# A branch projection of a macaron block as seven block products, with its weight sums made in DRAM

## The chip, the cores and the metric

One core of a Trainium2 chip runs the whole block in one launch. The metric is the device time in microseconds, as the median of several executions. The engines are named as the profile names them: PE multiplies matrices, ACT and DVE work on tiles in SBUF and PSUM, POOL here mostly clears tiles and issues a few transfers, SP issues nearly all transfers. Each engine, and each queue of transfers, takes its instructions in the order of the program.

## The reference

A layer on 256 tokens of width 1024: a gated feed-forward part, a mixer, a cross attention to 256 memory tokens, and a second feed-forward part, all in float32. The change touches the end of the mixer:

```python
o_a = rmsnorm(o_a.astype(x.dtype), hg_norm_g[l]) * jax.nn.silu(g_a)
y_a = o_a @ w_branch_a[l]
...
y_b = o_b.astype(x.dtype) @ w_branch_b[l]

gate = jax.nn.sigmoid((gates + b_gate[l]).astype(jnp.float32)).reshape(B, S, N_BRANCH, D)
y = (gate[:, :, 0] * y_a.astype(jnp.float32) + gate[:, :, 1] * y_b.astype(jnp.float32)).astype(x.dtype)
x = x + rmsnorm(y @ w_out[l], mix_post_g[l])
```

`o_a` and `o_b` are 256 x 1024, both branch matrices 1024 x 1024.

## The kernel before

**Weights.** Every matrix is cut into units of 128 x 1024 numbers (512 KB), two blocks of 128 x 512 each; a matrix of 1024 x 1024 has eight. `load_split` (L138) takes one unit through three steps: SP loads it into one of four `raw` tiles, ACT rounds it to `hi` (L147, the line of the cast), DVE takes `lo = raw - hi` (L149). There are eight `hi` and eight `lo` tiles. A product of float32 accuracy is made of three matmuls per block: hi times hi, hi times lo, lo times hi (`proj_tok`, L223). A weight tile comes free when PE has used it last, a `raw` tile when DVE has taken its `lo`.

**Order.** The kernel is written as one long sequence, but a list scheduler decides the order on each engine: by when operands are expected, by the number of buffers, and by marks in the code (`issue_after`, and `after(i)`, which ties work to the i-th matmul in a log). Once built, the order is fixed: an instruction that waits holds up all behind it on its engine.

**PSUM** has four `acc` banks, two `mm` banks and two `tr` banks of 128 x 512.

**The stages around the change, in PE's order.**

- `f_a`, `q_a` and so on (L844 on): the columns of the input projection. Before them `row_of` (L351) sends a column of norm factors through DRAM as a row and back to all partitions: two transfers on POOL (L356, L358); the row is first used on DVE at L861.
- `gates(c)` for c = 0 to 3 (L1252): the two branches' gates. Each chunk c has four units and, for the two halves h of the tokens, 24 matmuls into an `mm` bank, which DVE evicts into `zg` with a scale and the bias row `brow` (L1261). In the gaps of chunks 0 and 1 PE transposes the first branch's tokens into `OA` and makes the attention output `OB` (`fox_out`, L1222; its last split is the mark `OB`).
- `memT`, the memory tokens transposed, is scaled and split by eight ACT and eight DVE instructions (L366, L367).
- The sigmoid of the four gates (L1294), after the mark `OB`, in place; then `table`, which loads the ACT functions of the later stages.
- The branch loop (L1308): for c = 0, 1 (half of the output's columns) the first branch (`br_a` with `OA`), then the second (`br_b` with `OB`), each for both halves h: four units, twice 24 matmuls, 192 in all. DVE multiplies each `mm` bank by its gate (L1320) and adds the second branch to the first (L1323). `y_T` transposes the sum on PE and splits it, 16 matmuls (`L_Y`) into a later product.
- `rows_proj` (L1325) for `w_out`.

Other parts of the kernel (the feed-forward parts) already compute with seven block products.

Of the kernel before, what the change touches and what calls it, by code (L numbers as in the profile page):

```python
# [59 lines left out]
HX = T + 2 * KB  # L60

WARM = 8

X_AT = 12

# [17 lines left out]
def block_kernel(ctx: ExitStack, tc: tile.TileContext, wts, head_in, gf_in, x_in, mem_in, memT_in, cols, rows, fbias, masks, out):  # L83
# [12 lines left out]
    def MM(*args, **kw):  # L96
        log.append(PE.matmul(*args, **kw).ins)  # L97
# [9 lines left out]
    def nm(s):  # L107
        count[0] += 1
        return f"{s}_{count[0]}"

    def m4(shape, dt=F32, n="m"):
        return mp.tile(shape, dt, tag="m4", name=nm(n))
# [19 lines left out]

    place = {}

    def parts_of():
        return [wp.tile([P, D], F32R, tag=t, name=nm(t), bufs=8) for t in ("hi", "lo")]

    def load_split(src, n=512, behind=None, parts=None):  # L138

        raw = wp.tile([P, D], F32, tag="raw", name=nm("raw"), bufs=4)  # L140
        hi, lo = parts or parts_of()
        r, h, l = raw, hi, lo
        if n < 512:
            r, h, l = (p.rearrange("p (k n) -> p k n", k=2)[:, :, :n] for p in (raw, hi, lo))
        loads.append(nc.sync.dma_start(r, src).ins)
        with tc.issue_after(behind[0]) if behind else nullcontext():
            S.copy(h, r)  # L147
        with tc.issue_after(behind[1]) if behind else nullcontext():
            V.tensor_tensor(out=l, in0=r, in1=h.bitcast(F32), op=ALU.subtract)  # L149
        return hi, lo  # L150

    def unit(name, i):
        u = _AT[name] + i
        if u not in cache:
            cache[u] = load_split(wts[u - 4], behind=hold.get(u), parts=place.get(u))
        return cache[u]

    def chunk(name, c):
        return [unit(name, 4 * c + i) for i in range(4)]

    def blk(units, kb, n=512):
        hi, lo = units[kb // 2]
        o = (kb % 2) * 512
        return hi[:, o : o + n], lo[:, o : o + n]
# [124 lines left out]
    def table(ins):  # L289

        with tc.issue_after(ins):
            S.activation(warm, ones[:, 0:1], AF.Abs_reciprocal_sqrt)
# [461 lines left out]

    X1 = Joined()
    heads, raw1 = [], []
    for kb in range(KB):
# [492 lines left out]
    def gates(c):  # L1252
        u = chunk("gates", c)
        z = m4([P, 2, 512], n="zg")
        brow = wp.tile([P, D], F32, tag="extra", name=nm("brow"), bufs=4)[:, :512]
        with tc.issue_after(loads[-1]):
            nc.sync.dma_start(brow, rows[4 + c // 2, c % 2 * 512 : c % 2 * 512 + 512].partition_broadcast(P))
        for h in range(2):
            ps = mm()
            proj_tok(ps, X2, u, h)  # L1260
            V.scalar_tensor_tensor(out=z[:, h], in0=ps, scalar=r2[h], in1=brow, op0=ALU.mult, op1=ALU.add)  # L1261
        zs.append(z)
# [11 lines left out]
            fox_out(g)  # L1274


    memT_s = [m4([P, 4, T], n="memT") for _ in range(2)]
    for j in range(2):
        nc.sync.dma_start(memT_s[j], memT_in[:, 4 * j : 4 * j + 4, :])
# [9 lines left out]
    rowm = row_of(fac[1])  # L1289
    for c in range(2, 4):  # L1290
        gates(c)
    for c in (0, 2, 1, 3):
        with tc.issue_after(marks["OB"][0]):
            z_last = S.activation(zs[c], zs[c], AF.Sigmoid)  # L1294
    table(z_last.ins)
    g2 = load_row(1)
    Y = Pair()

    def y_T(c, h, m):

        tr = trp()
        with after(m):
            for i in range(4):
                PE.transpose(tr[:, i * P : (i + 1) * P], zs[c][:, h, i * P : (i + 1) * P], ident)
            hs = slice(h * P, (h + 1) * P)
            split(Y.h[c][:, :, hs], Y.l[c][:, :, hs], tr.rearrange("p (i t) -> p i t", i=4))

    for c in range(2):  # L1308
        for name, X, zc in (("br_a", OA, c), ("br_b", OB, 2 + c)):
            u = chunk(name, c)  # L1310
            for h in range(2):
                z = zs[zc][:, h]
                m = len(log)
                ps = mm()
                proj_tok(ps, X, u, h)
                if zc != c and h == 1:
                    y_T(c, 0, m + L_Y)
                if zc == c and h == 0 and c:
                    y_T(c - 1, 1, m + L_Y)
                V.tensor_tensor(out=z, in0=ps, in1=z, op=ALU.mult)  # L1320
                if zc != c:
                    za = zs[c][:, h]
                    V.tensor_tensor(out=za, in0=za, in1=z, op=ALU.add)  # L1323

    def rows_proj(ps, X, name, h, kbs, cols=(0, 1)):  # L1325
        a, b = h * P, h * P + P
# [246 lines left out]
```

## Time and profile before

| | us |
|---|---|
| median of three executions | 774.62 |
| lowest, highest | 774.27, 776.5 |
| the profiled execution | 776.3 |
| its span, first to last instruction | 774.0 |
| PE busy in the span | 764.9 |
| DVE busy | 647.6 |
| ACT busy | 493.2 |

The granted TensorE clock of the profiled execution was 0.998 of full speed. A share of busy time is an average over all stages; what a stage is bound by is read from that stage's window, and from what its engines waited for. In rows of groups the columns are busy time, mean ns of one, and idle time of the engine just before such instructions, with what ended most of it; in the timeline they are start, duration, instruction, and in brackets the idle time before it.

### The profile page before, as it was taken

To read this page: it belongs to the slowest core of one execution; us is meant where nothing else is said; L and a number is where in the kernel's file an instruction comes from. 1 tells how busy PE (TensorE), PEld (TensorE's weight loads), DVE (VectorE), ACT (ScalarE), POOL (GpSimd) and SP (SyncE) were. 2 spreads that over 40 slices of the span, in tenths; PEclk is the share of its full clock that TensorE was granted. 3 is DMA by queue.
4 is the path that set the end of the run, shared out by engine and by line. 5 is a ranking of instruction groups with operands and counts; after the bars stand their busy time and mean duration, and the time that the engine had idled before them with its cause. 6 is when DMAs were issued, how large, how long until landed. Compare 5 with 4: busy or idle time off the path is not lost.

```text
span 774.0 us, 11823 instructions
## 1 busy us (share of the span) xinstructions
PE 764.9 (99%) x4394; PEld 650.7 (84%) x4394; DVE 647.6 (84%) x992; ACT 493.2 (64%) x803; POOL 17.3 (2%) x39
## 2 busy tenths in 40 slices
PE   9999999999999999999999999999999999999996
PEld 8888888888888998898888888889888888888885
DVE  7798999997778898988776665886578999999993
ACT  7656564768775678557676444862668557665762
POOL 0000000000000101200000000000000000000000
PEclk9999999999999999999999999999999999999999
DMA  9748377255654545834667655456075736467241
GB/s 344 264 165 284 151 261 272 88 188 206 220 177 147 166 155 155 308 111 160 221 245 246 203 173 174 164 173 233 9 248 183 271 113 202 182 213 303 76 142 55
DMA packets 44505, 148.06 MB, mean 191 GB/s; under 512 B 5144, under 2 KB 8864, under 8 KB 44448
## 3 DMA queue, kind: packets, MB, share of 16 engines
q1 hardware_dynamic: 43168, 144.83, 54.0%
q0 software_dynamic: 848, 2.12, 1.1%
q8 instruction: 34, 0.56, 0.3%
q10 hardware_dynamic: 432, 0.37, 0.2%
q14 instruction: 23, 0.19, 0.1%
HBM read 146.24 MB, written 1.06 MB: 190 GB/s over the span
## 4 chain that ended last, share of the span: by engine, by line
PE 83%; DVE 9%; ACT 3%; DMA 2%; issue 1%; DVEq 0%; ACTq 0%; SPq 0%
PE mm L97 37%; PE acc L97 34%; PE tr L97 10%; DVE lo L149 3%; DMA raw<-in_wts_dram 2%; DVE lo L168 1%; ACT hi L147 1%; PE tr L379 1%; PE tr L438 1%; DVE k L986 1%; DVE qf L986 1%; ACT hi L167 1%; DVE xs L415 0%; ACT f L1024 0%; PE tr L1210 0%
## 5 line engine op out<-in xcount | busy, mean ns | idle before, releaser
L149 DVE TENSOR_TENSOR lo<-raw,hi 128x1024 fp32r<-128x1024 f32 (+1 forms) x212 | 251.5, 1202 | 36.9 <-ACT hi L147 31.7
L147 ACT CAST hi<-raw 128x1024 fp32r<-128x1024 f32 (+1 forms) x212 | 215.5, 1035 | 76.8 <-PE mm L97 38.0
L97 PE MATMUL mm<-hi,hlT 128*128 128x512 f32 (+1 forms) x624 | 190.5, 382 | 0.0
L97 PEld LDWEIGHTS mm<-hi,hlT 128*128 128x128 f32 x624 | 115.3, 188 | 19.8
L97 PE MATMUL mm<-lo,hlT 128*128 128x512 f32 (+1 forms) x312 | 117.5, 381 | 0.1
L97 PE MATMUL acc<-hi,act 128*128 128x512 f32 x352 | 113.3, 390 | 0.0
L97 PEld LDWEIGHTS acc<-hi,act 128*128 128x128 f32 x352 | 66.1, 188 | 13.6 <-ACT act L167 0.2
L97 PE MATMUL acc<-lo,act 128*128 128x512 f32 x176 | 69.3, 394 | 0.0
L167 ACT CAST hi<-sraw 128x1024 fp32r<-128x1024 f32 x50 | 52.0, 1055 | 27.0 <-DVE sraw L578 21.3
L97 PEld LDWEIGHTS mm<-lo,hlT 128*128 128x128 f32 x312 | 58.5, 188 | 10.0 <-DVE lo L149 0.5
L97 PE MATMUL acc<-hlT,hi 128*128 128x512 f32 x256 | 64.4, 393 | 0.0
L168 DVE TENSOR_TENSOR lo<-sraw,hi 128x1024 fp32r<-128x1024 f32 x50 | 60.3, 1219 | 0.5 <-ACT hi L167 0.4
L97 PEld LDWEIGHTS acc<-hlT,hi 128*128 128x128 f32 x256 | 46.1, 189 | 8.3
L97 PE MATMUL mm<-hlT,hi 128*128 128x512 f32 (+1 forms) x192 | 43.9, 357 | 0.0
L97 PE MATMUL tr<-hi,sx 128*128 128x512 f32 x120 | 39.3, 391 | 0.0
L97 PEld LDWEIGHTS acc<-lo,act 128*128 128x128 f32 x176 | 33.1, 188 | 7.2 <-DVE lo L149 0.7
L97 PEld LDWEIGHTS acc<-hlT,lo 128*128 128x128 f32 x256 | 35.0, 190 | 2.5
L97 PEld LDWEIGHTS mm<-hlT,hi 128*128 128x128 f32 x192 | 33.2, 189 | 4.3
L97 PE MATMUL acc<-hlT,lo 128*128 128x256 f32 x256 | 36.2, 283 | 0.0
L578 DVE TENSOR_TENSOR sraw<-sraw,raw 128x1024 f32<-128x1024 f32 x30 | 35.9, 1219 | 0.1
L97 PE MATMUL tr<-hlT,hi 128*128 128x512 f32 x128 | 32.6, 394 | 0.5 <-DVE act L168 0.5
L97 PE MATMUL mm<-hlT,lo 128*128 128x256 f32 x160 | 28.0, 285 | 1.1 <-DVE lo L149 1.1
(293 smaller groups left out, 1279.0 us busy)
## 6 DMA issues: line engine op xcount, KB each, us to landing
raw<-in_wts_dram SPq DMA_DIRECT2D x227, 512.0 KB, 4.3
sraw<-in_wts_dram SPq DMA_DIRECT2D x20, 512.0 KB, 5.5
raw<-in_gf_dram SPq DMA_DIRECT2D x12, 344.0 KB, 3.8
head<-in_head_dram SPq DMA_DIRECT2D x7, 392.0 KB, 6.6
grow<-in_rows_dram SPq DMA_DIRECT2D x4, 512.0 KB, 5.2
xs<-in_x_dram SPq DMA_DIRECT2D x2, 512.0 KB, 7.8
cbm<-cd POOLq DMA_DIRECT2D x2, 512.0 KB, 6.9
brow<-in_rows_dram SPq DMA_DIRECT2D x4, 256.0 KB, 3.7
```

The costliest lines, as they stand in the source:

```text
L97: log.append(PE.matmul(*args, **kw).ins)
L147: S.copy(h, r)
L149: V.tensor_tensor(out=l, in0=r, in1=h.bitcast(F32), op=ALU.subtract)
L167: a = S.copy(hi, src)
L168: b = V.tensor_tensor(out=lo, in0=src, in1=hi.bitcast(F32), op=ALU.subtract)
L379: PE.transpose(blocks[-1][1], src(kb), ident)
L438: PE.transpose(trv[:, j, h * P : (h + 1) * P], ats[c, h][:, j * P : (j + 1) * P], ident)
L578: V.tensor_tensor(out=x, in0=x, in1=y, op=ALU.add)
L986: V.tensor_tensor(out=tv, in0=tv, in1=other, op=ALU.mult)
```

## The change

The first branch's product, 256 x 1024 by 1024 x 1024, is taken as 2 x 2 blocks: tokens in halves (h), the contraction in halves (k), output columns in halves (c). Write x(h,k) for the four blocks of `o_a` and b(k,c) for those of the matrix. Instead of eight block products of 12 matmuls (two contracted blocks of 128 for each of the unit's two, three matmuls each) there are seven:

- p1 = x00 b00, copied to SBUF by ACT; the same bank then takes x01 b10 on top and is y00.
- p3 = (x01 - x00 + x10 - x11) b11
- q5 = (x10 - x11) s0, with s0 = b00 + b01
- q6 = (x00 - x10 + x11) s4, with s4 = s0 + b11
- p7 = (x00 - x10) s2, with s2 = b01 + b11; the same bank later takes x11 s6 on top, with s6 = s4 + b10
- v = p1 - q6 and w = q5 - v; then y11 = w - p7 (before x11 s6 is added), y01 = w + p3, y10 = v + p7, where y(h,c) has the rows h and columns c of the output.

**Sums of weights.** `plan` makes eight DRAM tiles (two units for each of s0, s2, s4, s6). `background` is called at every weight load; when the number of loads is one of 74, 78, ... 102, SP issues a copy from DRAM to DRAM of the one summand, and POOL a transfer that adds the other to it there, after the copy. s4 copies a finished s0, s6 a finished s4. In the program's order these fall into the stages from the first `f_a` weights to those of the `q_a` and `gf` stages, and `row_of`'s two transfers on POOL stand behind the third of the eight additions, the clearing of `aux` (L908) behind the eighth.

**Combinations of tokens.** After `fox_out`, on DVE: two additions of 128 x 1024 that join hi and lo of `OA`, four subtractions of 128 x 512; then two casts of 128 x 1024 on ACT and two subtractions on DVE for their hi and lo. They lie in two `raw` tiles and four `extra` tiles; `brow` of the gates 2 and 3 moves from `extra` to the pool `z2`.

**The branch loop.** Steps of `branch_pair`, a generator, alternate with the second branch's four products (c, h). The sigmoid of the fourth gate and the `table` load move out of the sigmoid loop, behind the second branch's second product in the text. Units loaded for the first branch go from 8 to 14: b00, b10, b11, s0, s4, s2, s6 with two units each.

```diff
+SUMS_AT = (*range(74, 103, 4),)
...
+    sums, jobs = [], []
+
+    def plan(name):
+        t = dp.tile([8, P, D + 16], F32, name=nm("sums"))
+        sums.extend(t[i, :, :D] for i in range(8))
+
+        def b(k, n, j):
+            return wts[_AT[name] + 4 * n + 2 * k + j - 4]
+
+        for j in range(2):
+            jobs.append((sums[j], b(0, 0, j), b(0, 1, j)))
+            jobs.append((sums[2 + j], b(1, 1, j), b(0, 1, j)))
+        for j in range(2):
+            jobs.append((sums[4 + j], sums[j], b(1, 1, j)))
+        for j in range(2):
+            jobs.append((sums[6 + j], sums[4 + j], b(1, 0, j)))
+
+    def background():
+        if jobs and len(loads) in SUMS_AT:
+            to, x, y = jobs.pop(0)
+            with tc.issue_after(loads[-1]):
+                nc.sync.dma_start(to, x)
+            G.dma_start(to, y, accum_op=ALU.add)
...
         loads.append(nc.sync.dma_start(r, src).ins)
+        background()
...
+    plan("br_a")
     X1 = Joined()
...
-        brow = wp.tile([P, D], F32, tag="extra", name=nm("brow"), bufs=4)[:, :512]
+        if c < 2:
+            brow = wp.tile([P, D], F32, tag="extra", name=nm("brow"), bufs=4)[:, :512]
+        else:
+            brow = sp.tile([P, 512], F32, tag="z2", name=nm("brow"), bufs=3)
...
+    fx, fh, fl = (
+        [wp.tile([P, D], dt, tag=tag, name=nm("fx"), bufs=4).rearrange("p (k t) -> p k t", k=4) for _ in range(2)]
+        for tag, dt in (("raw", F32), ("extra", F32R), ("extra", F32R))
+    )
+    for k in range(2):
+        V.tensor_tensor(out=fx[k], in0=OA.h[k].bitcast(F32), in1=OA.l[k].bitcast(F32), op=ALU.add)
+    fa_, fb_, fd_, fe_ = (fx[k][:, :, h * P : h * P + P] for h in range(2) for k in range(2))
+    V.tensor_tensor(out=fe_, in0=fd_, in1=fe_, op=ALU.subtract)
+    V.tensor_tensor(out=fd_, in0=fa_, in1=fd_, op=ALU.subtract)
+    V.tensor_tensor(out=fa_, in0=fa_, in1=fe_, op=ALU.subtract)
+    V.tensor_tensor(out=fb_, in0=fb_, in1=fa_, op=ALU.subtract)
+    for k in range(2):
+        S.copy(fh[k], fx[k])
+        V.tensor_tensor(out=fl[k], in0=fx[k], in1=fh[k].bitcast(F32), op=ALU.subtract)
+
+    def gated(c, h, x):
+        z = zs[c][:, h]
+        V.tensor_tensor(out=z, in0=x, in1=z, op=ALU.mult)
+
+    def plus(c, h):
+        V.tensor_tensor(out=zs[c][:, h], in0=zs[c][:, h], in1=zs[2 + c][:, h], op=ALU.add)
+
+    def branch_pair():
...
+        p1 = acc()
+        product(p1, of_x(0, 0), plain(0, 0), True)
+        p1s = half_tile("p1")
+        S.copy(p1s, p1)
+        product(p1, of_x(1, 0), plain(1, 0), False)
+        gated(0, 0, p1)
+        yield
+        p3 = acc()
+        product(p3, of(1, 0), plain(1, 1), True)
+        q5 = acc()
+        product(q5, of(1, 1), summed(0), True)
+        yield
+        q6 = acc()
+        product(q6, of(0, 0), summed(4), True)
+        with tc.high_priority():
+            v = less(p1s, q6)
+            w = less(q5, v)
+        p7 = mm()
+        product(p7, of(0, 1), summed(2), True)
+        with tc.high_priority():
+            gated(1, 1, less(w, p7))
+            gated(1, 0, less(w, p3, ALU.add))
+        yield
+        product(p7, of_x(1, 1), summed(6), False)
+        with tc.high_priority():
+            gated(0, 1, less(v, p7, ALU.add))
+            plus(0, 1)
+        yield
...
-    for c in (0, 2, 1, 3):
+    for c in (0, 2, 1):
         with tc.issue_after(marks["OB"][0]):
-            z_last = S.activation(zs[c], zs[c], AF.Sigmoid)
-    table(z_last.ins)
+            S.activation(zs[c], zs[c], AF.Sigmoid)
...
+    pair = branch_pair()
     for c in range(2):
-        for name, X, zc in (("br_a", OA, c), ("br_b", OB, 2 + c)):
...
+        u = chunk("br_b", c)
+        for h in range(2):
+            next(pair)
+            m = len(log)
+            ps = mm()
+            proj_tok(ps, OB, u, h)
+            if h == 1:
+                y_T(c, 0, m + L_Y)
+                if c == 0:
+                    with tc.issue_after(log[-1]):
+                        z_last = S.activation(zs[3], zs[3], AF.Sigmoid)
+                    table(z_last.ins)
+                else:
+                    y_T(0, 1, m + L_Y + 4)
+            gated(2 + c, h, ps)
+            if (c, h) != (0, 1):
+                plus(c, h)
```

`product` takes the three matmuls of each of its four blocks; `of` and `of_x` pick the block of the combined tokens or of `OA`; `summed` loads two units of a sum from DRAM with `load_split`, `plain` two units of the matrix; `less` subtracts (or adds) into a tile of 128 x 512.

More of the change, by code (lines that the diff above doesn't have):

```diff
@@ new lines, in branch_pair, with of, of_x, plain @@
+    def branch_pair():
+        assert not jobs
+        def of(k, h):
+            return lambda kk: (fh[k][:, kk, h * P : h * P + P], fl[k][:, kk, h * P : h * P + P])
+        def of_x(k, h):
+            return lambda kk: (OA.hi(4 * k + kk, h * P, h * P + P), OA.lo(4 * k + kk, h * P, h * P + P))
+        def plain(k, n):
+            return [unit("br_a", 4 * n + 2 * k + j) for j in range(2)]
+        def summed(i):
+            return [load_split(sums[i + j]) for j in range(2)]
+        def product(ps, stat, u, start):
+            for kk in range(4):
+                ah, al = stat(kk)
+                wh, wl = blk(u, kk)
+                for i, (x, y) in enumerate(((ah, wh), (ah, wl), (al, wh))):
+                    MM(ps, x, y, start=start and kk == 0 and i == 0, stop=kk == 3 and i == 2, skip_group_check=not start)
+        def half_tile(n):
+            return sp.tile([P, 512], F32, tag="z2", name=nm(n), bufs=3)
+        def less(x, y, op=ALU.subtract):
+            t = half_tile("br")
+            V.tensor_tensor(out=t, in0=x, in1=y, op=op)
+            return t
+        p1 = acc()
[26 more added lines that the diff above has]
+        yield
@@ L1306, in y_T @@
             split(Y.h[c][:, :, hs], Y.l[c][:, :, hs], tr.rearrange("p (i t) -> p i t", i=4))
+    pair = branch_pair()
     for c in range(2):
-        for name, X, zc in (("br_a", OA, c), ("br_b", OB, 2 + c)):
[L1310 to L1323, printed above, removed]
+        u = chunk("br_b", c)
[15 more added lines that the diff above has]
+                plus(c, h)
     def rows_proj(ps, X, name, h, kbs, cols=(0, 1)):
```

## The prediction

> **What bounds the kernel now.** I read the page's busy times and chain first, then what PE waited for, then the branch stage by windows.
>
> ```profile
> span 774.0 us, 11823 instructions
> PE 764.9 (99%) x4394; PEld 650.7 (84%) x4394; DVE 647.6 (84%) x992; ACT 493.2 (64%) x803; POOL 17.3 (2%) x39
> PE 83%; DVE 9%; ACT 3%; DMA 2%; issue 1%; DVEq 0%; ACTq 0%; SPq 0%
> ...
> engine line waited for: us in total, times, longest us
> PE mm L97 <- DVE lo L149: 1.1, 1, 1.1
> PE tr L97 <- PEq L1562: 0.8, 1, 0.8
> PE tr L97 <- DVE act L168: 0.5, 1, 0.5
> ```
>
> PE is busy for 764.9 of 774.0 us and its listed waits add up to 2.4 us. So the time is the number of matmuls times their pace, as long as nothing else falls behind; and a change can gain little except by dropping matmuls. The stage in question, from the first branch matmul to the first of w_out:
>
> ```profile
> core 0: us, PE busy (x) PEld busy (x) DVE busy (x) ACT busy (x) POOL busy (x), PEclk, DMA share, GB/s
> 170.00:250.00 80.00, 79.94 (x411) 67.73 (x410) 62.55 (x109) 55.05 (x100) 1.73 (x4) 1.00 0.59 194
> 360.00:400.00 40.00, 40.00 (x207) 33.72 (x206) 30.08 (x43) 27.58 (x49) 0.00 (x0) 1.00 0.66 229
> 417.60:461.10 43.50, 43.50 (x199) 35.97 (x198) 26.90 (x29) 19.45 (x20) 0.00 (x0) 1.00 0.58 195
> ...
> 10 pieces in order of time: start us, us, what
> 444.34 16.34 PE mm L97 x72
> ```
>
> From 417.6 to 461.1 PE is full at granted clock 1.00, DVE is busy for 26.9 of 43.5 us. One matmul takes 16.34/72 = 0.227 us, and the two branches' 192 take 43.6, the whole window. The window 360 to 400 is where the operands of the new products are made, 170 to 250 where the sums are made in DRAM.
>
> **What is removed.** Seven products of 12 matmuls replace eight for the first branch: 84 for 96, so 12 x 0.227 = 2.72 us less. PE is full here, so all of it counts: -2.72 us, 0.35 % of the time. That is the whole possible gain.
>
> **What is added: operands.** The new fx work is two additions and two subtractions for the lo part of 128x1024, four subtractions of half that size on DVE, and two casts on ACT. Nearest rows:
>
> ```profile
> L147 ACT CAST hi<-raw 128x1024 fp32r<-128x1024 f32 (+1 forms) x212 | 215.5, 1035 | 76.8 <-PE mm L97 38.0
> L578 DVE TENSOR_TENSOR sraw<-sraw,raw 128x1024 f32<-128x1024 f32 x30 | 35.9, 1219 | 0.1
> ...
> L149 DVE TENSOR_TENSOR lo<-raw,hi 128x1024 fp32r<-128x1024 f32 x33 | 40.1, 1221 | 10.0 <-ACT hi L147 8.8
> L1320 DVE TENSOR_TENSOR zg<-mm,zg 128x512 f32<-128x512 f32 x8 | 5.5, 688 | 8.5 <-PE mm L97 8.5
> L1323 DVE TENSOR_TENSOR zg<-zg,zg 128x512 f32<-128x512 f32 x4 | 2.8, 688 | 0.1
> ```
>
> DVE: 4 x 1.22 + 4 x 0.69 = 7.6 us; ACT: 2 x 1.04 = 2.1. In 360 to 400 DVE has 30.1 of 40 us, so 37.7 with it: it still fits behind PE as a sum, but everything behind it on DVE comes later, and the fx tiles hold two of the four raw buffers meanwhile, so weight loads start later too.
>
> The first thing late is an eviction. In the changed order on ACT and DVE the first half of the third gates chunk is evicted behind two casts, the sigmoid's table, one sigmoid, eight memT activations, a further cast and its subtraction; two mm banks exist, and the fourth chunk's first half needs that bank.
>
> ```profile
> 395.76 0.48 PE L97 MATMUL mm<-hi,hlT 128*128 128x512 f32 x1
> ...
> 396.04 0.59 ACT L167 CAST hT<-acc 128x512 fp32r<-128x512 f32 x1 [0.68 <-PE acc L97]
> 396.65 1.28 ACT L1294 ACT_TABLE_LOAD   x1
> 397.94 2.01 ACT L1294 ACTIVATE zg<-zg 128x1024 f32<-128x1024 f32 x2
> ...
> 399.86 1.69 ACT L366 ACTIVATE hlT<-memT,cols_s 128x256 fp32r<-128x256 f32 x4
> 401.77 1.71 ACT L366 ACTIVATE hlT<-memT,cols_s 128x256 fp32r<-128x256 f32 x4 [0.22 <-DMA memT<-in_memT_dram]
> ...
> 404.09 0.75 DVE L1261 SCALAR_TENSOR_TENSOR zg<-mm,facs,brow 128x512 f32<-128x512 f32 x1
> 404.76 3.49 DVE L149 TENSOR_TENSOR lo<-raw,hi 128x1024 fp32r<-128x1024 f32 x3
> ```
>
> The third chunk starts on PE at 395.76, so the fourth needs its bank 48 matmuls later, at 406.65; before, the eviction ended at 404.84, 1.8 us ahead. In the changed order the last hT cast ends at 396.63, then 2 x 1.04, 1.28, 1.06, 1.69 + 1.71, 1.04, a subtraction of 1.16 (3.49/3) and the eviction of 0.75: 407.4. That is 0.8 us late if the second of the two raw tiles is there; it waits for a raw buffer that fx or the previous chunk's last subtraction gives back at about 394 and lands 4.3 us later, at 398.3, its cast ending at 399.3 for 398.7: 0.6 more. Bounds 0 and 2.1 (memT landing later as well), taken 1.4: +1.4 us.
>
> **What is moved: the last sigmoid.** The sigmoid of the fourth gate chunk and the table load after it now stand on ACT between the casts of the first product's weights, with T the end of the gates on PE (417.6 before).
>
> ```profile
> 413.00 0.75 DVE L1261 SCALAR_TENSOR_TENSOR zg<-mm,facs,brow 128x512 f32<-128x512 f32 x1
> ...
> 418.69 0.75 DVE L1261 SCALAR_TENSOR_TENSOR zg<-mm,facs,brow 128x512 f32<-128x512 f32 x1
> ...
> 413.74 1.05 ACT L147 CAST hi<-raw 128x1024 fp32r<-128x1024 f32 x1 [2.37 <-PE mm L97]
> ...
> 419.47 1.06 ACT L1294 ACTIVATE zg<-zg 128x1024 f32<-128x1024 f32 x1 [0.59 <-DVE zg L1261]
> 420.54 1.28 ACT L292 ACT_TABLE_LOAD   x1
> ```
>
> DVE is through the fourth chunk's first eviction at 413.75, T-3.9. Then it has the other branch's three subtractions (3.5), four short steps of the norm (about 0.7) and the subtraction for the first product's first unit (1.2): done at T+1.5. PE wants it as its third matmul, at T+0.45: about 1.1 late. Behind it come the chunk's last eviction (T+2.3), the sigmoid (T+3.3) and the second unit's cast (T+4.4), wanted as the 15th matmul at T+3.2+1.1: 0.1 late, since PE now mixes the two branches' matmuls. The next unit's cast, the table, another cast and the copy of the first product (0.59) end at T+8.4; PE wants to go on in that bank at the 32nd matmul, T+7.0+1.2: 0.2. Together 1.4; before, the same sigmoid held up nothing, since the first branch's subtractions ran from 404.76 on. Bounds 0 (DVE reaches these subtractions early) and 2.0; taken 1.4.
>
> **The branch stage** has 22 subtractions and about 17 additions, products and splits: 22 x 1.22 + 17 x 0.69 = 38.6 us on DVE for 180 matmuls, 40.8 us; before it was 26.9 for 43.5. ACT's casts go from 16 to 22, 23 of 40.8 us: no bound. PE's weights thus arrive with little in hand, where the other branch's chunk keeps four of the eight hi/lo pairs. Each subtraction queued behind a sum that waits for a product's end can cost up to 1.2; I take 0.3 in all, bounds 0 and 3. The bias rows of the later gates from another pool and the moved transposes of y cost nothing: their number is the same, and the rows land like weights, in some 4 us, with a chunk (10.9 us of PE) in hand; without that cover, a late row would hold the same eviction as above.
>
> **Sums in DRAM.** Eight copies on SP and eight accumulating transfers on POOL, 512 KB each. No row shows either kind. Nearest rows:
>
> ```profile
> q1 hardware_dynamic: 43168, 144.83, 54.0%
> raw<-in_wts_dram SPq DMA_DIRECT2D x227, 512.0 KB, 4.3
> cbm<-cd POOLq DMA_DIRECT2D x2, 512.0 KB, 6.9
> ...
> 166.49 45.80 SPq L145 DMA_DIRECT2D raw<-in_wts_dram  x20
> ...
> 200.24 0.60 POOL L356 DMA_DIRECT2D rd<-runs  x1 [173.40 <-DVE runs L354]
> 204.29 0.56 POOL L358 DMA_DIRECT2D row<-rd  x1 [3.45 <-PE mm L97]
> ...
> 204.84 0.58 POOL L908 MEMSET aux<- 128x256 f32 x2
> ...
> 216.04 0.69 DVE L861 TENSOR_TENSOR f<-f,row 128x512 f32<-128x512 f32 x1
> ...
> L1010 DVE COPY_PREDICATED aux<-masks_s,acc x2: 442/445/448, 262.5 to 262.8; 128x256 f32<-128x256 int32 x2
> ```
>
> A load of 512 KB takes 0.54 x 774 x 0.524/144.83 = 1.5 us of all sixteen engines, so the sixteen transfers take 24 us, and 36 if reading both operands costs half as much again: 0.30 to 0.45 of the 80 us from 170 to 250, where the share is 0.59. Sum 0.89 to 1.04: full at worst, some 3 us of weights later. Half of the idle time ahead of all casts ends with PE (38.0 of 76.8 us on the page), so loads are there ahead of room for them, and I take 0, bounds 0 and 3. Two queues can stick. SP's fifth copy, about 40 us after the first, waits for the first accumulation: issued some 7 us after its copy (6.9 above, the slowest 512 KB row there), it has over 25 us in hand. On POOL the broadcast of the norm's row stands behind the third accumulation, which waits for a copy issued near 195, so it starts near 202 instead of 200.24; DVE needs the row at 216.04, and it landed about 4 us after 204.29: 8 us in hand for 2 lost. The clearing of aux, at 204.84 before, moves behind the last accumulation, near 252, and is wanted at 262.5.
>
> The page "DMA: Bandwidth & Descriptors" of the Trainium skill, section "Issuing engines are not separate DMA queues", says that transfers of any issuing engine run on the same sixteen engines and interleave, which speaks against calling POOL's transfers free; its section on the anatomy of one DMA would put one of 512 KB at 2.0 us + bytes/436e3 = 3.2 us, an estimate, and the sum would be the same.
>
> **Sum:** -2.72 + 1.4 + 1.4 + 0.3 = +0.4 us on the profiled execution's 776.3: 776.7. That execution lies 1.7 above the median 774.62, so on the median's footing 775.0. About 0.3 % (2.3 us) is what a measurement here can tell from no change.
>
> **Rivals.**
> 1. All of it hidden: DVE, with 10 us idle in 360 to 400, takes evictions in time and ACT's casts come early. For it: before, no wait in these stages. Against: 1.8 us in hand at the bank, of which the queue eats more. 774.62 - 2.7 = 771.9. Chance 0.22.
> 2. Slower, DVE becomes the bound of the branch stage: 38.6 of 40.8 us leaves 2.2 for its waits, and it had 8.5 us of them on PE alone in the old order (L1320 above). From 2.2 us of waits on it costs one for one; with half to all of 8.5, 2 to 6 us beside the likeliest case's sum: 777 to 781. Against: waits before came because it had nothing else to do. Chance 0.22.
> 3. Slower, the accumulations: where one takes over about 25 us, SP stops at the fifth copy with loads behind it; where the third is issued 8 us late, DVE stops at the row. Each us beyond that costs one; 3 to 10 give 778 to 785. Against: no 512 KB row is over 7 us. Chance 0.11.
> 4. That the change does not do what it says, with as many matmuls as before, 774.6: excluded, twelve are gone from PE's order.
>
> The page "SBUF — State Buffer" of the Trainium skill, section "Who interferes with whom", lets DVE block GpSimd's writing of transfer descriptors while it runs in its two-port modes; that would make rival 3's accumulations late, and no run here shows it.
>
> **Numbers.** The likeliest case has 0.45, 773.3 to 777. Below 772.3 (faster) lie rival 1 and a little of the likeliest: 0.24; above 776.9 rivals 2 and 3 and a little: 0.35; the rest, 0.41, is the same. The range 771.6 to 779.8 leaves out most of rival 3 and the ends of 1 and 2.
>
> **What would show it.** Branch matmuls over 40.8 us with PE full would bear out the gain. A PE wait on DVE's third-chunk eviction just before the fourth chunk, near 1.4 us, and one of about 1 us on the first product's lo, show the two stalls; if PE has no waits there and the time falls by 2.7, rival 1 is right. DVE busy for over 95 % of the branch stage with several PE waits on lo is rival 2; waits near 170 to 250, rival 3. A fall above 3 us, or a stall elsewhere, would make the working wrong.

## The result, and the profile after

The changed kernel takes 780.36 us in the median (775.13 to 786.21, 13 runs) against 775.5 for the kernel before in runs beside it (774.27 to 777.6, 13 runs): a ratio of 1.0054, 95 % interval 1.0037 to 1.0071. That is slower by about 0.5 %, or 4 us, though twelve matmuls are gone. The times also lie further apart than before, 11 us against 3: the seven executions at a mean granted clock of 0.998 or 0.999 took 775.1 to 780.4 us, the six at 0.993 to 0.996 took 781.0 to 786.2. The profiled execution took 782.04 us, 5.7 more than the profiled one before.

The page of the kernel after, rows as shown of before; in the rows of transfers the last number is us from issue to landing:

```profile
span 780.2 us, 11871 instructions
...
PE 766.4 (98%) x4382; PEld 649.5 (83%) x4382; DVE 663.0 (85%) x1011; ACT 500.8 (64%) x812; POOL 23.7 (3%) x47
...
PE 72%; DVE 11%; DMA 8%; ACT 4%; issue 4%; DVEq 0%; ACTq 0%; SPq 0%
...
L176 ACT CAST hi<-raw 128x1024 fp32r<-128x1024 f32 (+1 forms) x218 | 221.7, 1035 | 80.3 <-DMA raw<-in_wts_dram 46.0
...
raw<-in_wts_dram SPq DMA_DIRECT2D x225, 512.0 KB, 4.4
...
raw<-in_gf_dram SPq DMA_DIRECT2D x12, 344.0 KB, 6.3
sums<-in_wts_dram POOLq DMA_DIRECT2D x8, 512.0 KB, 8.0
...
sums<-in_wts_dram SPq DMA_DIRECT2D x4, 512.0 KB, 8.7
```

Three things are to be seen. PE runs 4382 matmuls instead of 4394 and is yet busy for 1.5 us more: some of them ran at a lower clock. In the chain that ended last, DMA has 8 % where it had 2 %. And the idle time of ACT ahead of the casts, before ended half by PE (38.0 of 76.8 us), now ends with a load in 46.0 of 80.3 us: loads are what comes last.

What PE waited for in the kernel after (us in total, times, longest us):

```profile
PE mm L99 <- ACT hlT L395: 1.3, 1, 1.3
PE acc L99 <- DVE lo L178: 1.2, 2, 0.8
PE mm L99 <- DVE lo L178: 1.0, 2, 0.5
PE tr L99 <- PEq L1680: 0.8, 1, 0.8
PE acc L99 <- DVE q L911: 0.7, 1, 0.7
PE mm L99 <- DVE hlT L396: 0.7, 1, 0.7
PE acc L99 <- DVE qf L1003: 0.5, 1, 0.5
PE mm L99 <- DVE zg L1294: 0.4, 1, 0.4
```

The waits on `hlT`, `q` and `qf` stand in stages whose computation the change does not touch. Comparing the times at which the same matmul starts in the two traces gives, stage by stage, what was lost (us, after less before): to the mixer's start (186) -0.7; to `f_a`'s start (209) +3.7; `f_a` to `gf` 0; the first `gf` stretch (254 to 264) +1.7; to the gates -0.6; gates 0 and +0.6; the branch stage 45.55 for 44.95, +0.6; from w_out to the end +0.8. So 5.4 of the 6.2 us by which the span grew are lost where the sums are made, over 150 us ahead of the branch stage.

Windows of the kernel after on the two lossy stages and the branch stage, then of the kernel before on the first two (columns as in the prediction's windows):

```profile
190.00:212.00 22.00, 20.07 (x85) 15.91 (x84) 14.16 (x26) 14.08 (x26) 2.01 (x3) 0.92 0.78 219
254.00:268.00 14.00, 12.78 (x258) 11.95 (x258) 12.42 (x21) 7.43 (x13) 2.25 (x7) 1.00 0.75 222
422.40:468.00 45.60, 43.87 (x194) 34.48 (x193) 37.40 (x42) 28.77 (x31) 0.81 (x2) 1.00 0.80 276
```

```profile
190.00:212.00 22.00, 21.94 (x104) 17.92 (x103) 17.17 (x29) 17.14 (x33) 1.73 (x4) 1.00 0.69 220
254.00:268.00 14.00, 14.00 (x271) 13.74 (x270) 13.47 (x22) 8.09 (x15) 2.66 (x12) 1.00 0.49 157
```

PE was full in both stretches before. Now it idles 1.93 us in the first and 1.22 in the second, and in the first its mean granted clock is 0.92.

**The first loss, step by step.** The timeline of ACT in the kernel after (start, duration, what, in brackets the idle time before it and what ended it):

```profile
194.17 0.19 ACT L316 ACTIVATION_READ_ACCUMULATOR junk<-xs 128x1 f32 x1
197.13 1.04 ACT L176 CAST hi<-raw 128x1024 fp32r<-128x1024 f32 x1 [2.76 <-DMA raw<-in_wts_dram]
198.08 0.29 ACT L339 ACTIVATE y<-ss,v 128x1 f32<-128x1 f32 x1
198.28 0.28 ACT L340 ACTIVATE v<-ss,v 128x1 f32<-128x1 f32 x1
198.46 0.60 ACT L395 ACTIVATE hlT<-tr,cols_s 128x128 fp32r<-128x128 f32 x2
```

And of PE:

```profile
197.21 0.39 PE L99 MATMUL mm<-hi,hlT 128*128 128x512 f32 x1
198.86 0.74 PE L99 MATMUL mm<-w,hlT 128*128 128x512 f32 x2 [1.26 <-ACT hlT L395]
200.26 4.04 PE L99 MATMUL mm<-w,hlT 128*128 128x512 f32 x10 [0.66 <-DVE hlT L396]
```

The cast at 197.13 is that of `f_a`'s second unit. Its load was issued at 189.86 and landed at 197.1, 7.2 us later where a load takes 4.3 before. PE wants this unit only at 212.9, so the load has over 14 us in hand. But the cast stands in ACT's fixed order ahead of the activations that make `hlT` of the second half of the tokens, and PE wants those at 197.6. ACT waits 2.76 us for data that nobody wants yet, and PE stands still behind it. After that the clock falls, in narrow windows of the kernel after:

```profile
196.00:200.00 4.00, 2.33 (x9) 1.25 (x8) 1.41 (x3) 1.94 (x5) 0.00 (x0) 1.00 0.99 381
200.00:204.00 4.00, 3.74 (x10) 3.01 (x11) 2.75 (x11) 2.45 (x7) 1.42 (x2) 0.62 1.01 302
204.00:206.00 2.00, 2.00 (x9) 1.62 (x9) 0.00 (x0) 0.18 (x1) 0.00 (x0) 0.90 0.78 141
```

The lost clock costs 4 x 0.38 + 2 x 0.10 = 1.7 us; with 1.93 idle that is 3.6 of the stage's 3.7.

**The second loss** has the same form. ACT, then PE, of the kernel after:

```profile
259.00 0.77 ACT L176 CAST hi<-raw 128x688 fp32r<-128x688 f32 x1 [1.31 <-DMA raw<-in_gf_dram]
259.68 0.36 ACT L248 COPY plo<-acc 128x256 f32<-128x256 f32 x1
261.92 0.63 ACT L910 ACTIVATE q<-z 128x512 f32<-128x512 f32 x1 [1.88 <-DVE z L909]
```

```profile
263.33 0.46 PE L99 MATMUL acc<-q,k 128*32 128x32 f32 x32 [0.72 <-DVE q L911]
...
264.59 0.46 PE L99 MATMUL acc<-qf,early 128*32 128x32 f32 x32 [0.49 <-DVE qf L1003]
```

A cast of a `gf` unit waits 1.31 us for its load. Behind it stand the copy `plo`, then over DVE `z`, then the sigmoid `q`, which PE wants. PE waits 0.72 and 0.49 us.

### The profile page after: what moved, and what is told of

Read it like the earlier page. It is cut to its first block, busy times and chain, and to the rows that moved or that the text cites. A ratio compares the mean times of both kernels' runs of the same rounds, so it can differ in the third digit from the quotient of the medians.

```text
span 780.2 us, 11871 instructions
## 1 busy us (share of the span) xinstructions
PE 766.4 (98%) x4382; PEld 649.5 (83%) x4382; DVE 663.0 (85%) x1011; ACT 500.8 (64%) x812; POOL 23.7 (3%) x47
## 4 chain that ended last, share of the span: by engine, by line
PE 72%; DVE 11%; DMA 8%; ACT 4%; issue 4%; DVEq 0%; ACTq 0%; SPq 0%
PE acc L99 30%; PE mm L99 30%; PE tr L99 10%; DMA raw<-in_wts_dram 4%; DVE lo L178 4%; DMA raw<-in_gf_dram 2%; DVE lo L197 2%; ACT hi L176 2%; DMA raw<-sums 1%; PE tr L467 1%; PE tr L408 1%; DVE qf L1016 1%; DVE k L1016 1%; ACT hlT L395 1%; ACT f L1054 0%
## 5 line engine op out<-in xcount | busy, mean ns | idle before, releaser
L178 DVE TENSOR_TENSOR lo<-raw,hi 128x1024 fp32r<-128x1024 f32 (+1 forms) x218 | 258.6, 1201 | 38.0 <-ACT hi L176 34.4
L176 ACT CAST hi<-raw 128x1024 fp32r<-128x1024 f32 (+1 forms) x218 | 221.7, 1035 | 80.3 <-DMA raw<-in_wts_dram 46.0
```

## The experiments

The twelve runs asked three things: what the transfers cost alone and through what (E2, E3, E5, E6, E11), what the branch stage costs without them (E1, E4, E7, E9, E10), and whether the parts add up (E0, E8). Ratios are to the kernel before in runs beside it, with 95 % intervals; stage figures are differences to the kernel before, from one profile each.

**E0, the same kernel again.**

> The changed kernel once more, for its spread. Both theories: about 780 us, ratio 1.004 to 1.007. Transfers theory (the sums' transfers make weight loads late between 186 and 270 us): the profile again shows PE idle for 1 to 3 us between 190 and 210, and again a granted clock under 1.00 right behind it; how much varies from run to run, and with it the time. Branch theory (operand work and the branch stage cost it): PE's loss between 190 and 210 is a chance of one run and is gone here, with the time still near 780.

1.0081 [1.006, 1.0102], 781.98 us. The profiled execution took 786.25 us, the most of its six, and lost at the same two places: +4.3 at `f_a` and +4.5 in `gf`. There the cast waits 2.82 us for its load instead of 1.31, and now the clock falls behind it as well; windows of E0:

```profile
262.00:266.00 4.00, 1.77 (x102) 1.44 (x100) 2.77 (x5) 1.97 (x4) 1.13 (x3) 1.00 0.98 204
266.00:270.00 4.00, 3.29 (x102) 3.10 (x103) 3.96 (x7) 1.41 (x3) 0.00 (x0) 0.57 0.72 207
```

So the loss differs between these two executions with how late the loads land, and a late load that leaves PE idle long enough also costs a stretch at half clock.

**E1, the branch as changed, without the sums in DRAM.** The second, fourth, sixth and seventh products read plain units of the matrix.

```diff
-    plan("br_a")
...
         def summed(i):
-            return [load_split(sums[i + j]) for j in range(2)]
+            w = {0: 0, 4: 2, 2: 4, 6: 6}[i] + _AT["br_a"] - 4
+            return [load_split(wts[w + j]) for j in range(2)]
```

> The changed kernel without its sixteen background transfers; the products that need sums load plain units of the same matrix instead, so the output is not the reference's, and the branch stage has the same loads and matmuls. Transfers theory: 774.5 to 776.5 us, ratio 0.999 to 1.001, with PE full and clock 1.00 between 180 and 270. Branch theory: 779 to 781, unchanged.

1.0012 [1.0, 1.0023]. PE is full from 190 to 212 and both lossy stages are gone (-0.4 and 0). The branch stage takes 45.43 us against 44.95. So without one background transfer the twelve matmuls' 2.72 us still do not appear.

**E2, the kernel before with the sixteen transfers, which nobody reads.** `plan` and `background` are added to the kernel before, and nothing else.

```diff
+SUMS_AT = (*range(74, 103, 4),)
...
         loads.append(nc.sync.dma_start(r, src).ins)
+        background()
...
+    plan("br_a")
     X1 = Joined()
```

> The kernel before with only the sixteen background transfers added, at the same loads; nobody reads the sums. Transfers theory: 779 to 782 us, ratio 1.005 to 1.008, with PE idle between 190 and 210. Branch theory: 775 to 776, ratio 1.000.

1.0038 [1.0023, 1.0053], some 3 us, a little less than the transfers theory gave. The transfers alone cost that, and with E1 it adds up: 0.38 + 0.12 = 0.50 % against 0.54 (0.81 in E0). The profile puts 1.6 of its 2.6 us in the `f_a` stage again. Accumulations took 6.8 us there in the median, copies of a matrix unit 5.4 and copies of a sum 6.6.

**E3, the same transfers at other places,** two groups: under the first feed-forward part, and under the attention and the gates.

```diff
-SUMS_AT = (*range(74, 103, 4),)
+SUMS_AT = (58, 59, 64, 65, 131, 132, 138, 140)
```

> The changed kernel with the sums' transfers at other loads: the first four at loads 58, 59, 64 and 65 (about 115 to 150 us), the others at 131, 132, 138 and 140 (about 337 to 385 us), stretches with DMA shares of 0.2 to 0.5. Transfers theory: 774 to 777 us, ratio 0.998 to 1.002, PE full between 190 and 270. Branch theory: 779 to 781.

1.0064 [1.0046, 1.0083]: no better. `f_a` (-0.4) and `gf` (0) lose nothing, but 1.7 us are lost ahead of 186, 1.7 in the gates, and the branch stage takes 49.4, 4.4 more, part of it at a granted clock of 0.72 (448 to 454). Ahead of the branch the loss goes with the transfers. In the branch, where no sum is made any more, PE waits twice for a cast, 2.9 us in all, and on ACT the casts there had waited 1.46 us (the one of 422.14) and 2.55 us (of 444.54) for their loads. The half clock behind the second wait costs another 1.7 us. Why these loads come so late is not settled.

**E4, E1 with the other branch's second chunk loaded later,** so that the products' own units come first.

```diff
     for c in range(2):
-        u = chunk("br_b", c)
         for h in range(2):
+            if (c, h) == (0, 0):
+                u = chunk("br_b", c)
             next(pair)
+            if (c, h) == (1, 0):
+                u = chunk("br_b", c)
```

> The changed kernel without background transfers (as before: plain units in place of sums, output not the reference's), and with the four units of the second branch's second half loaded after those of q6 and p7 instead of ahead of them. Order theory (in the branch stage the weights of q6 and p7 come late because four units that PE needs 12 us later stand ahead of them in the queues of loads, casts and subtractions): PE's loss between 430 and 460, 2.1 us without the sums, falls under 0.8, and the ratio from 1.0012 to 0.998 to 0.9995. DVE theory (the stage has too much work on DVE, 38.6 of 40.8 us): the loss stays near 2 and the ratio near 1.001.

1.0015 [1.0004, 1.0027], the same as E1 and what the DVE theory gave. No weight is late for PE in the branch stage any more; instead it waits for an evicted bank. That row of E4's waits of PE:

```profile
PE mm L99 <- DVE zg L1328: 2.3, 1, 2.3
```

The branch stage took 46.6 us, with a stretch at clock 0.57 (456 to 460) behind that wait; the wait and the lost clock are 4 us of it. DVE is busy for 19.05 of the 19.1 us from 442.5 to 461.6, and the eviction stands in that full queue behind subtractions and sums. So in this order it is DVE that holds PE up, where in E1's order it is the weights.

**E5, the change with the two casts held behind the urgent work.** The loads stay where they are; only ACT's order changes (and DVE's at `gf`).

```diff
+    hold[_AT["f_a"] + 1] = evicted[-1]
     row2 = row_of(fac[0])
...
-            S.activation(qj, z, AF.Sigmoid)
-            V.tensor_tensor(out=qj, in0=qj, in1=z, op=ALU.mult)
+            q_sig = S.activation(qj, z, AF.Sigmoid).ins
+            q_mul = V.tensor_tensor(out=qj, in0=qj, in1=z, op=ALU.mult).ins
...
-        u = [load_split(gf_in[4 * c + i], GF) for i in range(4)]
+        u = [load_split(gf_in[4 * c + i], GF, behind=(q_sig, q_mul) if (c, i) == (1, 3) else None) for i in range(4)]
```

> The changed kernel with all its transfers, where two casts on ACT are put behind what they held up: that of f_a's second unit behind the last normalized block before it, that of the gf unit 7 behind the last plo and sigmoid of q_a. Queue theory (a cast that waits for a late load holds up on ACT what PE needs at once; the weights themselves would be early enough): PE's losses at 196 to 204 and 262 to 266 fall under 0.4 us each, the granted clock there stays 1.00, ratio 1.000 to 1.003 for 1.006 to 1.008. Bandwidth theory (the weights themselves come too late for PE): the losses move some us on, ratio 1.005 to 1.008.

1.0048 [1.0031, 1.0064]; the profile lies 5.0 us over the kernel before. At `f_a` the hold does what it should. E5's window and, in a second fence, its ACT:

```profile
190.00:212.00 22.00, 22.00 (x107) 18.43 (x106) 14.52 (x27) 14.78 (x28) 2.06 (x3) 1.00 0.91 259
```

```profile
196.61 2.38 ACT L395 ACTIVATE hlT<-tr,cols_s 128x128 fp32r<-128x128 f32 x6 [0.40 <-PE tr L408]
198.89 0.68 ACT L854 ACTIVATE iv<-mm,facs 128x512 f32<-128x512 f32 x1
199.46 0.62 ACT L395 ACTIVATE hlT<-tr,cols_s 128x128 fp32r<-128x128 f32 x2
199.96 1.06 ACT L176 CAST hi<-raw 128x1024 fp32r<-128x1024 f32 x1
```

The same transfers run in these 22 us, the DMA share is higher than in the kernel after (0.91 against 0.78), and PE is full at clock 1.00: -0.4 us instead of +3.7. The loads are as late as before: the two issued behind that of `f_a`'s second unit land after 5.4 and 6.9 us in both traces. So what turned a late load into 3.7 us was the place of a cast in ACT's queue. At `gf` it does not work: 2.3 us are still lost, 1.21 of them in a wait of PE on `qf`, and on DVE the held `lo` (0.88 us) now stands right ahead of `qf`. The gates (+1.2) and the branch stage (+1.5) are longer as well, and the median gains nothing beyond its interval.

**E6, E5 with E4's order.** The edits of both.

> The changed kernel with both edits, all its transfers and the reference's output: the two casts behind what they held up, and the second branch's second half loaded after q6 and p7. Queue and order theory together: 0.997 to 1.001, at the best 2 us faster than before. If the sums' transfers cost by bandwidth or DVE bounds the branch stage: 1.003 to 1.008.

1.0053 [1.0032, 1.0075], 776.75 to 782.92. In the profile, of an execution of 778.92 us, `f_a` is at -0.4 again, `gf` at +2.6, the branch at +0.2, where PE waits 1.6 us for an evicted bank as in E4.

**E7, E4 with the other branch's eight `lo` subtractions on POOL,** to take load from DVE.

```diff
-            V.tensor_tensor(out=l, in0=r, in1=h.bitcast(F32), op=ALU.subtract)
+            (eng or V).tensor_tensor(out=l, in0=r, in1=h.bitcast(F32), op=ALU.subtract)
...
-            cache[u] = load_split(wts[u - 4], behind=hold.get(u), parts=place.get(u))
+            cache[u] = load_split(wts[u - 4], behind=hold.get(u), parts=place.get(u), eng=G if name == "br_b" else None)
```

> The kernel without transfers and with the second branch's second half loaded later (as e4: plain units in place of sums, output not the reference's), and the eight subtractions for the second branch's lo moved from DVE to POOL. DVE theory (DVE's queue, with 22 subtractions and 17 sums in some 41 us, makes evictions and weights late in the branch stage): the stage, from the first product's first matmul to w_out's first, shortens from 45.4 to 46.6 us towards 43, PE's loss between 430 and 460 falls under 0.8, ratio 0.996 to 1.000. Load theory (four raw tiles, each taken for a landing, a cast and a subtraction, are the limit): the stage stays over 45, ratio 1.000 to 1.003. If POOL takes over 5 us for one subtraction, or slows DVE, the stage grows.

1.0088 [1.0073, 1.0103], clearly worse: the branch stage takes 53.4 us, with a wait of 3.5 us of PE on an evicted bank and two stretches of half clock in a row, 6.8 us, that cost 3.4.

**E8, all of it together:** the change with the holds, E4's order and POOL's subtractions (the hold at `gf` on ACT alone, for two units).

> The changed kernel with all transfers and the reference's output: f_a's second cast behind the normalized blocks, the casts of gf's units 3 and 7 behind the sigmoids of q_a's second and fourth product pair, the second branch's second half loaded later, its eight subtractions on POOL. Queue theory: no loss of PE over 0.5 us between 190 and 270. With DVE theory as well: ratio 0.996 to 0.999, faster than both kernels. With load theory in the branch stage: 0.999 to 1.002. If the transfers cost by bandwidth: 1.004 or more.

1.01 [1.0085, 1.0114], the slowest. `gf` is down to +0.9, but the branch takes 50.6 us. What a subtraction costs on POOL, and one of DVE's beside it, from E8:

```profile
L178 POOL TENSOR_TENSOR lo<-raw,hi 128x1024 fp32r<-128x1024 f32 x8 | 19.7, 2490 | 107.6 <-ACT hi L176 107.6
```

```profile
452.13 2.33 DVE L178 TENSOR_TENSOR lo<-raw,hi 128x1024 fp32r<-128x1024 f32 x1 [3.78 <-ACT hi L176]
```

On POOL it takes 2.49 us for DVE's 1.22, so a `raw` tile is held longer, and DVE waits 3.78 us for a cast; that the one causes the other is likely, but was not tried apart. DVE's own subtraction at 452.13 took 2.33 us; POOL was subtracting until 453.38. The page "SBUF — State Buffer" of the Trainium skill, section "Who interferes with whom", says that a DVE instruction with two inputs in SBUF and a GpSimd instruction that reads SBUF contend for a shared port, which is locked for a whole instruction. The trace agrees: 1.25 us are lost to POOL's end, and 1.08 are left for work that takes 1.22 alone. Earlier in E8 a DVE instruction on 128x1, of 0.22 us alone, took 2.32 us beside another of POOL's subtractions (412.5 to 414.9), while DVE's evictions, with one input in PSUM, kept their 0.74 us.

**E9, E1 with ten units instead of fourteen for the seven products.** The second product uses the third block's units, the seventh those of the sixth; the matmuls and all of DVE's sums stay.

```diff
+        kept = []
+
         def summed(i):
             w = {0: 0, 4: 2, 2: 4, 6: 6}[i] + _AT["br_a"] - 4
-            return [load_split(wts[w + j]) for j in range(2)]
+            if i == 0:
+                return plain(1, 1)
+            if i != 2:
+                kept[:] = [load_split(wts[w + j]) for j in range(2)]
+            return kept
```

> The kernel without transfers (as e1), where q5 takes the units that p3 has loaded and p7 those of q6: ten units are loaded for the first branch instead of 14, with as many matmuls and sums; the output is not the reference's. Supply theory (each further unit takes a raw tile for a landing, a cast and a subtraction, and the stage is limited by how fast units come): the branch stage, 45.4 us without the transfers, falls to 42.2 to 43.5, ratio 0.997 to 0.999. Sums theory (DVE's sums between the subtractions hold up banks and weights): it stays over 44.5, ratio 1.000 to 1.002.

0.9976 [0.9967, 0.9984], the only kernel of the twelve faster than before, 773.71 against 775.59. The branch stage takes 42.5 us, 2.4 less than before, and PE has no wait in it. Its window in E9:

```profile
417.40:460.00 42.60, 42.60 (x194) 34.82 (x194) 33.79 (x38) 25.00 (x27) 0.80 (x2) 1.00 0.75 251
```

**E10, E1 with the sums of the products on 64 of 512 columns,** so that DVE is free of most of that work.

```diff
-        z = zs[c][:, h]
-        V.tensor_tensor(out=z, in0=x, in1=z, op=ALU.mult)
+        z = zs[c][:, h, :64]
+        V.tensor_tensor(out=z, in0=x[:, :64], in1=z, op=ALU.mult)
...
-            V.tensor_tensor(out=t, in0=x, in1=y, op=op)
+            V.tensor_tensor(out=t[:, :64], in0=x[:, :64], in1=y[:, :64], op=op)
```

> The kernel without transfers (as e1) with its 14 units, where the gate products and the sums of the branch stage on DVE work on 64 of 512 columns, in the same order but for a few places; the output is not the reference's. Sums theory: the branch stage falls from 45.4 us to 42.2 to 43.5, ratio 0.997 to 0.999. Supply theory: it stays over 44.5, since units come no faster, ratio 1.000 to 1.002. Both: 43.5 to 44.5.

1.0027 [1.0018, 1.0035], no better than E1, though DVE is down to 32.5 of 46.2 us in the branch stage (37.6 of 45.4 in E1, 33.8 of 42.6 in E9). A stretch at a granted clock of 0.85 and 0.72 (4 us each from 440) costs 4 x 0.15 + 4 x 0.28 = 1.7 us of it; without that the stage would be 0.9 us shorter than E1's, so in this order DVE's sums explain at most that of some 3. PE's waits in the branch stage, in E1 and then in E10, of which the two longer ones stay:

```profile
PE acc L99 <- ACT hi L176: 0.8, 1, 0.8
PE acc L99 <- DVE lo L178: 0.8, 1, 0.8
PE mm L99 <- DVE lo L178: 0.5, 1, 0.5
```

```profile
PE acc L99 <- ACT hi L176: 0.9, 1, 0.9
PE acc L99 <- DVE lo L178: 0.8, 1, 0.8
```

Fewer units bring the gain, less work on DVE little. The row of the casts within the branch stage, by instructions of one form, says why (at the end the idle time ahead of them, and what ended most of it), in the kernel before, the kernel after, E1 and E9, a fence for each:

```profile
L147 ACT CAST hi<-raw 128x1024 fp32r<-128x1024 f32 x16 | 16.9, 1056 | 19.3 <-PE mm L97 19.2
```

```profile
L176 ACT CAST hi<-raw 128x1024 fp32r<-128x1024 f32 x24 | 25.0, 1051 | 15.2 <-DMA raw<-sums 6.3 <-DMA raw<-in_wts_dram 4.7 <-PE mm L99 3.5
```

```profile
L176 ACT CAST hi<-raw 128x1024 fp32r<-128x1024 f32 x24 | 25.0, 1050 | 15.1 <-DMA raw<-in_wts_dram 8.7 <-PE mm L99 3.6 <-PE tr L1419 2.8
```

```profile
L176 ACT CAST hi<-raw 128x1024 fp32r<-128x1024 f32 x20 | 20.9, 1052 | 15.9 <-PE mm L99 9.3 <-DMA raw<-in_wts_dram 4.4 <-PE acc L99 2.2
```

Before, a cast waited for PE to give a weight tile back: the supply was ahead of the demand. In the kernel after and in E1 it waits mostly for a load (11.0 of 15.2 us, 8.7 of 15.1): the demand has caught up with the supply. In E9 it waits mostly for PE again.

**E11, E5 with the holds at `gf` on ACT alone, for the last unit of the first two `gf` chunks.**

```diff
-        u = [load_split(gf_in[4 * c + i], GF, behind=(q_sig, q_mul) if (c, i) == (1, 3) else None) for i in range(4)]
+        u = [load_split(gf_in[4 * c + i], GF, behind=(q_sigs[2 * c + 1], None) if c < 2 and i == 3 else None) for i in range(4)]
```

> The changed kernel with all transfers and the reference's output, with three casts held back: f_a's second, and gf's units 3 and 7 behind the sigmoids of q_a's second and fourth pair. Queue theory: PE loses under 0.6 us between 190 and 270, and the time is that of the kernel without transfers to within 1 us, ratio 1.001 to 1.003. Bandwidth theory: a loss of over 1.5 us there, ratio over 1.004.

1.0053 [1.0036, 1.007], 777.7 to 782.55. The profiled execution has the lowest of these times; it has +1.7 at `gf`, and 1.9 us in all over the kernel before. By its number the loss at `gf` is what the bandwidth theory gave; in the trace PE waits 1.21 us there on `qf`, again behind the `lo` of the held cast on DVE. That the loss at `gf` is one of queues is thus argued from timelines: no hold removed it. No trace shows where the executions with longer times lose. The hold at `f_a` thus removes its stall in each of the four profiles that have it (E5, E6, E8, E11), but no version here beats the kernel before and computes the block.

## Why the prediction was right or wrong, step by step

The forecast was 775.0, no change that can be told; it came out slower by 0.54 %, on the prediction's footing 1.0054 x 774.62 = 778.8: inside the range, but as the case that was given 0.35, not the 0.41 of no change. That the range holds it is partly luck: the two stalls of 1.4 us each came out at some 0.4 and 0, while two terms taken at 0 and 0.3 measured some 3 us each. The prediction says that a stall elsewhere would make the working wrong, and the two at `f_a` and `gf` are such stalls. By its own steps:

**What bounds the kernel, and -2.72: right.** PE is the bound, and where its weights arrive in time the twelve matmuls are worth that: E9's branch stage is 2.4 us shorter. Its total of -0.24 % (1.9 us) is the most that any version here brought. The window of the prediction ends at 461.10; w_out's first matmul starts at 462.57, since the stage also has twelve short transposes, hence 44.95 us here.

**"I take 0" for the sums in DRAM: the step that failed.** It measured 0.38 % alone (E2), 2.9 us, next to its upper bound of 3, and 5.4 us in the profile of the kernel after. The price of the transfers was about right: 8.0 and 8.7 us each for an assumed 7, and a DMA share of 0.86 from 170 to 250 where 0.89 to 1.04 was worked out. The false premise was "loads are there ahead of room for them", drawn from the idle time ahead of all casts on the page. That is a total, and it says nothing of the one cast that stands ahead of an urgent instruction on ACT. The prediction asked what is queued behind a waiting instruction on SP and on POOL ("Two queues can stick"), but not on ACT. E5 shows it for `f_a`: same transfers, that cast moved, stall gone. Nor was the fall of the clock in the sum; it makes 1.7 of the 3.7 us in the profile.

**SP's fifth copy and the norm's row: right, and harmless.** The copy was issued at 214.08 without a wait; the row's transfer left at 208.79 instead of 204.29 and landed at 216.44, 5 us ahead of DVE's use at 221.7. Rival 3 gave 778 to 785, which holds the result, and waits near 170 to 250 as its sign, which came; its mechanism, a late accumulation that stops SP or DVE, did not occur.

**+1.4 at the gates' bank: right place, a third of the size.** PE waits 0.4 on that eviction (last row of the waits above), the stage that follows is 0.6 longer, and 0.7 in E1. The queue ahead of that eviction, from the end of the last `hT` cast (400.96) to the eviction's (411.29), took 10.3 us where 10.8 was worked out, since each instruction starts some 0.1 us before the one ahead of it ends. The 0.6 us for a `raw` tile that comes late did not occur: ACT runs there without a gap.

**+1.4 for the late sigmoid and subtraction: 0 in the kernel after.** From 420 to 430 PE is full there. DVE reached these subtractions early, the lower bound. In E7 and E8, with the other branch's subtractions on POOL, 0.85 us of the stall appears.

**+0.3 for the branch stage: too small by a factor of ten.** Against 44.95 - 2.72 = 42.2 us it takes 45.55 with the sums and 45.43 without, 3.3 and 3.2 more, just over the bound of 3. The prediction looked to DVE's 38.6 of 40.8 us for the cause, as rival 2 did. Rival 2's sign, DVE over 95 % busy in the stage, did not come (37.4 of 45.6 us). E10 takes most of the sums off DVE and gains 0.9 at most; E9 takes four units away and gains nearly all. What runs out in this order is the supply of units: 22 in place of 16 through four `raw` tiles, each held from the issue of its load to the end of its subtraction, at a DMA share of 0.80 where it was 0.59. The prediction had "ACT's casts go from 16 to 22 ... no bound", which is true of ACT's time and misses the loads ahead of it. Within the supply, whether landing times or the number of `raw` tiles counts most was not tried apart. With the loads in E4's order the weights come in time and DVE's queue holds up a bank instead, so rival 2 is not far off; E10's lighter sums in E4's order were not run.

**Left open.** With the stall at `f_a` gone (E5, E11) the medians do not fall beyond their intervals, and only part of that is seen: E5's profile still loses at `gf`, in the gates and in the branch stage, while E11's is its fastest execution, and no trace shows where the others lose. Why loads come late in E3's branch stage is not explained.

## What to carry to other kernels

Before adding background transfers, look not at the mean slack of the loads but at each in-order engine: which instruction waits for a load, and what urgent work stands behind it; slack of the data itself (14 us here) protects nothing. Trading matmuls for more weight data pays only while the supply keeps ahead, which the idle time ahead of the casts showed here: ended by PE, there was room; ended mostly by loads, there was none. Taking load off an engine that is merely busy is worth little (E10), and work moved to a slower engine can hold a shared buffer for longer (E7).

## What the runs showed of the hardware

- **The clock falls behind a stretch of 3.41 us with about half of it idle.** In the traces each half-clock stretch ahead of a kernel's end lasts 3.41 us (6.83 in E7), starts a whole multiple of 3.413 us after the start of full clock, and costs 1.7 us (3.4 in E7, where the window from 464 to 468 has a clock of 0.50). Laid out on this grid, the stretches in which PE idled 1.59 us (E10), 1.92 (E3), 1.93 (the kernel after), 2.33 (E4), 2.48 and 2.71 (E0) and 2.58 (E7) were each followed by half clock. Those with 1.56 us (E8, twice), 1.53 (E3) or less were not. So it counts where idle time falls: in E8 PE idles for 3.1 of 4 us, half of it in each of two stretches, and the clock stays:

```profile
458.00:462.00 4.00, 0.88 (x4) 0.59 (x4) 3.65 (x6) 2.90 (x3) 0.00 (x0) 1.00 0.84 316
```

The page "TensorE: Matmul & The Clock Gate" of the Trainium skill, section "Part 1: The HAM clock gate", puts the halved clock behind an idle window of about 3.4 us that runs freely. The halved clock, its length and the free run agree. That idle time shorter than one window was enough differs, and here the measurement decides.
- **An accumulating transfer in DRAM** of 512 KB took 8.0 us in the median (6.8 in E2) and a copy within DRAM 8.7 of a matrix unit and 8.1 of a sum (5.4 and 6.6 in E2), where a load to SBUF took 4.3 to 4.4. Beside them others' loads were slower: those of `gf` (344 KB) went from 3.8 to 6.3 us.
